# The first half of x squared, normed and turned block by block into eight PSUM banks, with three weight chunks rounded behind it

## The chip, the cores and the metric

The kernel runs on one core of a Trainium2 chip. The metric is the device time of one execution in microseconds, measured on several executions; the lower the better. The core has a matrix engine (PE, whose weight loads the profile lists apart as PEld), a vector engine (DVE), a scalar engine (ACT), a general engine (POOL) and a queue engine that issues most transfers (SP). Each works through its own queue in order and waits at an instruction until what it needs is there. Matrix results go to PSUM, which has eight banks of 128 x 512 f32 values.

## What is computed

One layer of a decoder step: a half-step SwiGLU FFN, a token mixer (a pooling branch and an SSD branch, gated and merged), a second half-step FFN, a last norm, for 1024 prompt tokens and 64 sample tokens of width 1024. The change concerns only the start of the first FFN:

```python
def rmsnorm(x, g):
    xf = x.astype(jnp.float32)
    y = xf * lax.rsqrt(jnp.mean(xf * xf, axis=-1, keepdims=True) + EPS)
    return (y * g.astype(jnp.float32)).astype(x.dtype)

def swiglu(x, w_in, w_out):
    gu = x @ w_in
    g, u = gu[..., :D_FF], gu[..., D_FF:]
    return (jax.nn.silu(g) * u) @ w_out

x = x + 0.5 * swiglu(rmsnorm(x, norm_ffn1[l]), ffn1_w_in[l], ffn1_w_out[l])
```

## The kernel before

**Halves, blocks, k.** The tokens are worked on in two halves: h = 0 has 512 prompt tokens, h = 1 has 512 prompt tokens and the 64 samples. x lies in memory token by token, and the products want it with the channels on the partitions. So `load_x(h, out)` loads a half in blocks of 128 tokens, each as two tiles of 512 channels (`xin`), and turns it on PE: eight slices k of 128 channels, each a PSUM bank (`ptx`) of 128 channels x 512 tokens. The norm rides along: the right operand of the turning matmul is a diagonal matrix `dg` with the reciprocal root mean square of each token.

**Steps of load_x before.** ACT squares all eight tiles and sums each row into `ss` (L911). Then, once for all blocks: DVE adds the two column halves (L914) and scales (L915), POOL takes the power -0.5 (`rsqrt`, L377), DVE makes one diagonal for each block (L921). Then for each k: four turns into one bank (L930), ACT writes the scaled slice `xn` (L934), DVE writes its rounded form `hi` (L935), and `lo = xn - hi` goes to DVE for even k and POOL for odd k (L940). hi and lo of half 0 share a tile named `hl`. Banks come from a pool of eight, split into six of tag `pd` for products and two of tag `ps` for the rest; the turns use `ps`, so at most two slices are under way.

**Products.** Every f32 product is made of three passes on rounded operands: hi x wh, lo x wh, hi x wl. `load_w` (L284) loads a chunk of weights (four slices of k, 128 columns) into `wraw`; ACT rounds it to `wh` (L307) and DVE makes the remainder `wl` (L308). There are three buffers each for `wh` and `wl`. Half 0 does its first three column blocks of the FFN plainly (`ffn_in_plain`, L626), half 1 its first two; for each k the plain code makes six passes, three into `pg` and three into `pu`. The other blocks use a scheme with seven products for a 2 x 2 split, whose operands are sums of slices: `combine` (L508) makes them with subtractions on POOL (L520) and splits them with ACT (L528) and DVE (L529).

**What sets the order.** The program is written as generators ("chains") with due times counted in matmul time; `tick` steps those that are due. Behind that a list scheduler orders each engine's instructions by priority, with a higher priority where the code says `tc.high_priority`, and a semaphore guards each true dependency. `hold` (L280) is a tiny POOL copy out of `ss` into a tile that is about to be loaded; it keeps a load back until that value is there. The second half's x and the weight chunks of k = 4 to 7 are held back in this way by the first half's `ss`.

**The start.** The main program opens the stage, steps `load_x` of half 0 five times, loads the first four weight chunks (`ahead`, the first chunk's key being (0, 0)), then starts `load_x` of half 1.

Of the kernel before, what the change touches and what calls it, by code (L numbers as in the profile page):

```python
# [21 lines left out]
NS = NB * NT  # L22
EPS = 1e-6
# [7 lines left out]
NTOK = (512, 576)  # L31
# [43 lines left out]
def tile_hybrid_pool_ssd_macaron(  # L75
# [10 lines left out]
    V, S, T, G = nc.vector, nc.scalar, nc.tensor, nc.gpsimd  # L86
# [12 lines left out]
    def act(shape=(P, 576), dt=F32, name="a"):  # L99
        return sp.tile(list(shape), dt, tag="act", bufs=N_ACT, name=nm(name))  # L100
# [20 lines left out]
    def fx(dt=F32, name="x"):  # L121
        if stage["name"] == "mix":
            return act((P, 576), dt, name)
        return stage["p"].tile([P, 592], dt, tag="fx", bufs=N_FX, name=nm(name))

    def psum(tag="ps", name="ps"):
        npd = stage["npd"]
        return stage["ps"].tile([P, 512], F32, tag=tag, bufs=npd if tag == "pd" else 8 - npd, name=nm(name))
# [46 lines left out]
    def mm(out, lhsT, rhs, start=True, stop=True, free=False):  # L175
        T.matmul(out, lhsT, rhs, start=start, stop=stop, skip_group_check=free)  # L176
        pe[0] += max(out.free_size(), 64) / 2400.0 * (1 if rhs.dtype == F32R else 4)
# [11 lines left out]
    ident = cp.tile([P, P], F32, tag="ident", name="ident")  # L189
# [50 lines left out]
    late = []  # L240
# [40 lines left out]

        G.tensor_copy(t[:1, :1], src)

    def load_w(w, k0, nk, c0, ncol=P, behind=None, keep=False):  # L284

        if (k0, c0) in ahead:
            return ahead.pop((k0, c0))
        if (w.tensor.name, k0, c0) in parted:
            nth[0] += 1
            out = []  # L290
            for t, src in zip(("wh", "wl"), parted[w.tensor.name, k0, c0]):
                if nth[0] % 2:
                    o = sp.tile([P, 4 * P], F32, tag="wraw", bufs=N_RAW, name=nm(t)).bitcast(F32R)
                else:
                    o = sp.tile([P, 4 * P], F32R, tag=t, bufs=N_W, name=nm(t))
                o = o[:, : nk * P]
                dma(o.bitcast(F32), src)
                out.append(o.rearrange("p (k c) -> p k c", c=ncol))
            return tuple(out)
        raw, wh, wl = (sp.tile([P, 4 * P], d, tag=t, bufs=n, name=nm(t))[:, : nk * ncol]  # L300
                       for t, d, n in (("wraw", F32, N_RAW), ("wh", F32R, N_W), ("wl", F32R, N_W)))
        if behind is not None:
            hold(raw, behind)
        dma(raw.rearrange("p (k c) -> p k c", c=ncol),
            w[k0 * P : (k0 + nk) * P, c0 : c0 + ncol].rearrange("(k p) c -> p k c", p=P))
        with tc.high_priority(hp[0]):
            S.activation(wh, raw, AF.Copy)  # L307
            V.tensor_tensor(wl, raw, wh.bitcast(F32), op=ALU.subtract)  # L308
        if keep:
            to = [dp.tile([P, nk * P], F32, tag=nm("part"), name=nm("part")) for _ in range(2)]  # L310
            for a, b in zip(to, (wh, wl)):
                dma(a, b.bitcast(F32))
            parted[w.tensor.name, k0, c0] = to
        return wh.rearrange("p (k c) -> p k c", c=ncol), wl.rearrange("p (k c) -> p k c", c=ncol)
# [60 lines left out]
    def rsqrt(r, ss):  # L375

        G.tensor_tensor(r, ss, mhalf[: ss.shape[0], : ss.shape[1]], op=ALU.pow)  # L377
# [510 lines left out]
    def load_x(h, out):  # L888


        N = NTOK[h]
        blocks = blocks_of(h)
        nb = len(blocks)
        ss = small((P, 4, 5), "xss", 2)
        if h == 1:
            G.memset(ss, 1.0)
        raws = []
        for src, _, c in blocks:
            raws.append([])
            for q in range(2):  # L900
                t = act((P, 512), name="xin")
                if h == 1:
                    hold(t, late[0][:1, 0, :1])
                dma(t[:c, :], src[:, q * 512 : (q + 1) * 512])
                raws[-1].append(t)
        late.append(ss)
        yield X1_AT if h else 0.2
        for i, (_, c0, c) in enumerate(blocks):
            for q in range(2):
                junk = act((P, 512), name="junk")  # L910
                S.activation(junk[:c], raws[i][q][:c], AF.Square, accum_out=ss[:c, q, i : i + 1])  # L911
            yield 0.5
        v = ss[:, 0, :nb]
        V.tensor_tensor(v, v, ss[:, 1, :nb], op=ALU.add)  # L914
        V.tensor_scalar(v, v, 1.0 / D, EPS, op0=ALU.mult, op1=ALU.add)  # L915
        rsqrt(ss[:, 2, :nb], v)
        yield 0.5
        dg = act((P, 576), name="dg")
        dg = [dg[:, i * P : i * P + b[2]] for i, b in enumerate(blocks)]
        for i, (_, c0, c) in enumerate(blocks):  # L920
            V.tensor_scalar_mul(dg[i][:c, :c], ident[:c, :c], ss[:c, 2, i : i + 1])  # L921
        if h == 1:
            pq = psum("ps", "pxs")
            for k in range(KD):
                mm(pq[:, k * NS : (k + 1) * NS], raws[4][k // 4][:NS, (k % 4) * P : (k % 4 + 1) * P], dg[4][:NS, :NS])
        hi, lo, xn, hl = [None] * KD, [None] * KD, [None] * KD, [None] * KD
        for k in range(KD):
            pt = psum("ps", "ptx")
            for i in range(4):
                mm(pt[:, i * P : (i + 1) * P], raws[i][k // 4][:, (k % 4) * P : (k % 4 + 1) * P], dg[i])  # L930
            x = fx(name="xn") if k >= 4 else act((P, 576), name="xn")
            a, b, both = (act((P, 576), F32R, "hi"), act((P, 576), F32R, "lo"), None) if h else pair(576)
            g = cols[:, i_g1 + k : i_g1 + k + 1]
            S.activation(x[:, :512], pt, AF.Copy, scale=g)  # L934
            V.tensor_scalar_mul(a[:, :512], pt, g)  # L935
            if h == 1:
                ps_ = pq[:, k * NS : (k + 1) * NS]
                S.activation(x[:, 512:N], ps_, AF.Copy, scale=g)
                V.tensor_scalar_mul(a[:, 512:N], ps_, g)
            (G if k % 2 else V).tensor_tensor(b[:, :N], x[:, :N], a[:, :N].bitcast(F32), op=ALU.subtract)  # L940
            hi[k], lo[k], xn[k], hl[k] = a, b, x, both
            yield 0.9
        out.append((h, hi, lo, xn, hl))
# [407 lines left out]
    st = open_stage("ffn1", N_PDF)  # L1351
    finish(start(load_cols(0, nr0)))
    prep1 = [(start(load_x(h, o)), o) for h, o in ((0, []), (1, []))]
    for _ in range(5):
        prep1[0][0].step()
    for kb in (0, 4):
        for c0 in (0, FF):
            ahead[kb, c0] = load_w(wi1, kb, 4, c0, behind=late[0][:1, 0, :1] if kb else None)
    prep1[1][0].step()

    def turn():
# [600 lines left out]
```

## Time and profile before

| what | us |
|---|---|
| median of three runs | 2876.56 (2874.2 to 2882.31) |
| the profiled execution | 2876.81 |
| its span | 2875.0 |
| PE busy | 2777.4 |
| last square of the first half ends, 12.04 + 0.19 | 12.23 |
| first turn on PE | 14.28 |
| first product on PE | 19.80 |
| first turn of the second half (pxs) | 36.77 |
| first plain product of the second half | 75.30 |

The span is the time from the first to the last instruction in the profile; the time of the execution has about 1.8 us more around it. All times in the views are counted from the span's start. In an order of time a row gives the start, the duration, the engine, the line, the operation, the tile written and those read, a count, and in brackets the idle time ahead of it with what ended it.

### The profile page before, as it was taken

How to read it: one execution, taken by the hardware profiler on the slowest of the kernel's cores; microseconds unless marked ns; L12 is line 12 of the kernel's file. 1: busy time of each engine (PE TensorE's matmuls, PEld its weight loads, DVE VectorE, ACT ScalarE, POOL GpSimd, SP SyncE). 2: the span in 40 equal slices, each digit the busy share in tenths (PEclk: the TensorE clock that was granted, in tenths of full speed). 3: DMA queues.
4: the chain of work that ended last, by engine and by line, in shares of the span. 5: the costliest groups of instructions: out<-in, count | busy, mean ns of one | idle time of the engine just before them, and what ended most of it. 6: DMA issues, size and time to landing. Idle time of an engine off the chain costs nothing. (4 is left out here: it accounts for less than half of the span.)

```text
span 2875.0 us, 54724 instructions
## 1 busy us (share of the span) xinstructions
PE 2777.4 (97%) x19834; PEld 2600.5 (90%) x19834; DVE 1887.1 (66%) x2912; ACT 1411.0 (49%) x3150; POOL 1377.5 (48%) x1406
## 2 busy tenths in 40 slices
PE   7999999999999999999999999899999999999998
PEld 5999999899889999999998887678999999998997
DVE  6655565777884586877776777866665544457776
ACT  5444444543454565554556566566233344435433
POOL 5566567543442365554632333333225766664432
PEclk9999999999999999999999999899999999999999
DMA  4565554797745455554367578786675323337865
GB/s 130 185 209 191 175 161 151 248 294 250 238 128 159 152 168 170 176 159 137 99 231 231 188 231 252 231 260 199 226 253 168 121 91 98 99 111 255 289 208 183
DMA packets 515792, 539.50 MB, mean 188 GB/s; under 512 B 41780, under 2 KB 356008, under 8 KB 515512
## 3 DMA queue, kind: packets, MB, share of 16 engines
q1 hardware_dynamic: 515504, 535.99, 58.1%
q8 instruction: 156, 2.56, 0.4%
q14 instruction: 116, 0.95, 0.1%
q10 hardware_dynamic: 16, 0.00, 0.0%
HBM read 383.43 MB, written 152.65 MB: 186 GB/s over the span
## 5 line engine op out<-in xcount | busy, mean ns | idle before, releaser
L176 PE MATMUL pw<-X,wh 128*128 128x288 f32 (+2 forms) x2832 | 626.3, 310 | 4.3 <-ACT v L575 2.7
L176 PEld LDWEIGHTS pw<-X,wh 128*128 128x128 f32 x2832 | 461.5, 189 | 26.4 <-ACT v L575 3.3
L176 PE MATMUL pw<-X,wl 128*128 128x288 f32 (+1 forms) x1644 | 473.1, 288 | 0.6 <-DVE wl L458 0.6
L458 DVE TENSOR_TENSOR wl<-s,wh 128x512 fp32r<-128x512 f32 x288 | 245.8, 855 | 245.2 <-ACT wh L457 232.5
L176 PE MATMUL pw<-hl,wh 128*128 128x256 f32 (+1 forms) x1536 | 393.1, 329 | 3.7 <-ACT t L579 2.5
L451 POOL TENSOR_TENSOR s<-wraw,wraw 128x512 f32<-128x512 f32 x144 | 198.2, 1376 | 330.6 <-DVE wl L458 214.4
L176 PE MATMUL pw<-hi,wh 128*128 128x288 f32 x1120 | 331.7, 296 | 1.8 <-DVE t L615 1.0
L176 PE MATMUL pw<-hi,wl 128*128 128x288 f32 x1120 | 329.8, 294 | 0.0
L176 PE MATMUL pw<-lo,wh 128*128 128x288 f32 x1120 | 329.7, 294 | 0.0
L176 PEld LDWEIGHTS pw<-X,wl 128*128 128x128 f32 x1644 | 311.1, 189 | 0.8 <-DVE wl L458 0.8
L176 PE MATMUL pw<-hl,wl 128*128 128x256 f32 x1072 | 301.4, 281 | 1.2 <-DVE wl L458 1.2
L176 PEld LDWEIGHTS pw<-hl,wh 128*128 128x128 f32 x1536 | 259.5, 190 | 25.3 <-ACT t L579 3.2
L758 POOL TENSOR_TENSOR ws<-wraw,wraw 128x512 f32<-128x512 f32 x120 | 177.5, 1486 | 200.5 <-DMA wraw<-in_ffn_w_out_dram 88.7
L458 DVE TENSOR_TENSOR wl<-wraw,wh 128x512 fp32r<-128x512 f32 x216 | 179.9, 833 | 125.1 <-ACT wh L457 121.4
L457 ACT ACTIVATE wh<-s 128x512 fp32r<-128x512 f32 x288 | 181.0, 629 | 136.1 <-PE pw L176 110.1
L176 PEld LDWEIGHTS pw<-hi,wh 128*128 128x128 f32 x1120 | 210.5, 188 | 8.7 <-DVE t L615 1.7
L457 ACT ACTIVATE wh<-wraw 128x512 fp32r<-128x512 f32 x216 | 135.6, 628 | 154.1 <-PE pw L176 132.8
L176 PEld LDWEIGHTS pw<-lo,wh 128*128 128x128 f32 x1120 | 210.6, 188 | 0.0
L176 PEld LDWEIGHTS pw<-hi,wl 128*128 128x128 f32 x1120 | 210.1, 188 | 0.0
L176 PEld LDWEIGHTS pw<-hl,wl 128*128 128x128 f32 x1072 | 203.8, 190 | 2.2 <-DVE wl L458 2.2
L176 PE MATMUL po<-hh,wh 128*128 128x272 f32 x848 | 178.7, 292 | 8.2 <-ACT wh L766 6.9
L176 PE MATMUL pso<-yhl,wh 128*128 128x288 f32 (+1 forms) x768 | 178.0, 337 | 5.0 <-ACT acc L1752 4.4
(402 smaller groups left out, 6826.8 us busy)
## 6 DMA issues: line engine op xcount, KB each, us to landing
wraw<-in_ffn_w_out_dram SPq DMA_DIRECT2D x240, 256.0 KB
wraw<-in_ffn_w_in_dram SPq DMA_DIRECT2D x188, 256.0 KB
wraw<-in_w_in_dram SPq DMA_DIRECT2D x144, 256.0 KB
wh<-part SPq DMA_DIRECT2D x116, 256.0 KB
wl<-part SPq DMA_DIRECT2D x116, 256.0 KB
hr<-xq SPq DMA_DIRECT2D x106, 272.0 KB
xq<-s SPq DMA_DIRECT2D x66, 272.0 KB
xq<-g SPq DMA_DIRECT2D x62, 272.0 KB
```

The source lines that it names most:

```text
L176: T.matmul(out, lhsT, rhs, start=start, stop=stop, skip_group_check=free)
L451: G.tensor_tensor(t, a, b, op=op)
L457: S.activation(wh, a, AF.Copy)
L458: V.tensor_tensor(wl, a, wh.bitcast(F32), op=ALU.subtract)
L758: G.tensor_tensor(s, raws[0], raws[1], op=ALU.subtract if p in MINUS2 else ALU.add)
```

## The change

Half 0 no longer waits for all its squares. In the order of the blocks, ACT squares a block's two tiles, DVE and POOL make the statistics for that block's single column of `ss`, DVE makes its diagonal, and PE turns all eight slices of this block into eight banks at once: six of tag `pd` and two of tag `ps`. So the eight banks are taken until the slices are read, and the first products take the banks of the first slices. The rest of `load_x` (scaling, hi, lo) becomes a function, `leave_x`, which both halves use; half 1 keeps the old order of work. The first weight chunk is now loaded behind one step of the chain, and the rounding of the second to the fourth chunk is pinned to program order.

```diff
-    def load_w(w, k0, nk, c0, ncol=P, behind=None, keep=False):
+    def load_w(w, k0, nk, c0, ncol=P, behind=None, keep=False, pin=lambda i: i):
...
-            S.activation(wh, raw, AF.Copy)
-            V.tensor_tensor(wl, raw, wh.bitcast(F32), op=ALU.subtract)
+            pin(S.activation(wh, raw, AF.Copy))
+            pin(V.tensor_tensor(wl, raw, wh.bitcast(F32), op=ALU.subtract))
...
         late.append(ss)
         yield X1_AT if h else 0.2
+        if h == 0:
+            pts = [psum("pd" if k < 6 else "ps", "ptx") for k in range(KD)]
+            for i in range(4):
+                cut = slice(i, i + 1)
+                for q in range(2):
+                    junk = act((P, 512), name="junk")
+                    S.activation(junk, raws[i][q], AF.Square, accum_out=ss[:, q, cut])
+                V.tensor_tensor(ss[:, 2, cut], ss[:, 0, cut], ss[:, 1, cut], op=ALU.add)
+                V.tensor_scalar(ss[:, 2, cut], ss[:, 2, cut], 1.0 / D, EPS, op0=ALU.mult, op1=ALU.add)
+                rsqrt(ss[:, 3, cut], ss[:, 2, cut])
+                dg = act((P, P), name="dg")
+                V.tensor_scalar_mul(dg, ident, ss[:, 3, cut])
+                for k in range(KD):
+                    mm(pts[k][:, i * P : (i + 1) * P], raws[i][k // 4][:, (k % 4) * P : (k % 4 + 1) * P], dg)
+                yield 0.5
+            yield from leave_x(h, out, pts, None)
+            return
...
-    for _ in range(5):
+    prep1[0][0].step()
+    first_w = load_w(wi1, 0, 4, 0)
+    for _ in range(4):
         prep1[0][0].step()
+    ahead[0, 0] = first_w
     for kb in (0, 4):
-        for c0 in (0, FF):
-            ahead[kb, c0] = load_w(wi1, kb, 4, c0, behind=late[0][:1, 0, :1] if kb else None)
+        for c0 in (FF,) if kb == 0 else (0, FF):
+            ahead[kb, c0] = load_w(wi1, kb, 4, c0, behind=late[0][:1, 0, :1] if kb else None,
+                                pin=tc.keep_in_program_order)
```

The scheduler's order changes with it, on every engine, up to about a tenth of the program; behind that the rows of every engine are the same again.

On PE, at the start of the program, the rows before were these; xin are the tiles of x, ptx the banks of turned slices, and pg and pu the first products.

```order
L176 MATMUL ptx_527<-dg_502,xin_421 128x128
L176 MATMUL pg_588<-hl_513,wh_442 128x512 x2
L176 MATMUL pg_588<-hl_513,wl_443 128x512
L176 MATMUL ptx_537<-dg_502,xin_409 128x128
L176 MATMUL ptx_537<-dg_502,xin_413 128x128
L176 MATMUL ptx_537<-dg_502,xin_417 128x128
L176 MATMUL ptx_537<-dg_502,xin_421 128x128
L176 MATMUL pu_589<-hl_513,wh_448 128x512
```

With the change, the same place on PE, the last block's turns and the first products, reads:

```order
L176 MATMUL ptx_431<-dg_497,xin_421 128x128
L176 MATMUL ptx_432<-dg_497,xin_421 128x128
...
L176 MATMUL ptx_437<-dg_497,xin_423 128x128
L176 MATMUL ptx_438<-dg_497,xin_423 128x128
L176 MATMUL pg_600<-hl_560,wh_426 128x512
L176 MATMUL pu_601<-hl_560,wh_508 128x512
L176 MATMUL pg_600<-hl_560,wh_426 128x512
L176 MATMUL pg_600<-hl_560,wl_427 128x512
```

Before, the last five slices were turned between products; now all 32 turns stand ahead of the first product, and no turn of this half stands behind it.

On POOL, in the stretch in which PE does the first plain block, the rows before were these; hl written from xn is the lo of an odd k (523 is k = 1, 543 k = 3, 563 k = 5), and the others are subtractions of `combine`.

```order
L940 TENSOR_TENSOR hl_523<-xn_522,hl_523 128x512
L520 TENSOR_TENSOR xn_522<-xn_522 128x256
L520 TENSOR_TENSOR xn_532<-xn_532 128x256
L940 TENSOR_TENSOR hl_543<-xn_542,hl_543 128x512
L520 TENSOR_TENSOR xn_542<-xn_542 128x256
L940 TENSOR_TENSOR hl_563<-xn_562,hl_563 128x512
```

With the change, POOL's rows from the lo of k = 3 (575) to that of k = 5 (585) are:

```order
L966 TENSOR_TENSOR hl_575<-xn_574,hl_575 128x512
L520 TENSOR_TENSOR xn_559<-t_74_615,xn_559 128x256
L520 TENSOR_TENSOR xn_564<-t_84_659,xn_564 128x256
L520 TENSOR_TENSOR xn_569<-xn_569 128x256
L520 TENSOR_TENSOR xn_574<-xn_574 128x256
L520 TENSOR_TENSOR t_102_734<-xn_589,xn_569 128x256
L520 TENSOR_TENSOR xn_569<-t_102_734,xn_569 128x256
L966 TENSOR_TENSOR hl_585<-xn_584,hl_585 128x512
```

One subtraction stood between these two lo; now six do. Four subtractions stand between the lo of k = 1 and that of k = 3 where two stood, and two stand between k = 5 and k = 7.

On ACT, where the second half is squared (junk), the rows before ended like this; wh are rounded weight chunks, X operands of the seven products.

```order
L911 ACTIVATE junk_623,xss_467<-xin_487 128x512
L307 ACTIVATE wh_461<-wraw_460 128x512
L911 ACTIVATE junk_625,xss_467<-xin_490 128x512
L911 ACTIVATE junk_630,xss_467<-xin_493 64x512
L911 ACTIVATE junk_632,xss_467<-xin_496 64x512
L528 ACTIVATE X_645<-xn_512 128x256
L307 ACTIVATE wh_844<-wraw_843 128x512
```

With the change, ACT's rows at the first squares of the second half are:

```order
L307 ACTIVATE wh_521<-wraw_520 128x512
L307 ACTIVATE wh_812<-wraw_811 128x512
L928 ACTIVATE junk_632,xss_527<-xin_529 128x512
L928 ACTIVATE junk_634,xss_527<-xin_532 128x512
L528 ACTIVATE X_638<-xn_559 128x256
L928 ACTIVATE junk_644,xss_527<-xin_535 128x512
L307 ACTIVATE wh_818<-wraw_817 128x512
L928 ACTIVATE junk_646,xss_527<-xin_538 128x512
```

Before, all ten squares of the second half stood ahead of the second block's weights (wh_844); now the second block's two first chunks (wh_812 and wh_818) stand ahead of ten and of seven of them.

More of the change, by code (lines that the diff above doesn't have):

```diff
@@ L921, in load_x, with turned @@
             V.tensor_scalar_mul(dg[i][:c, :c], ident[:c, :c], ss[:c, 2, i : i + 1])
[L922 to L926, printed above, removed]
+        pq = psum("ps", "pxs")
         for k in range(KD):
+            mm(pq[:, k * NS : (k + 1) * NS], raws[4][k // 4][:NS, (k % 4) * P : (k % 4 + 1) * P], dg[4][:NS, :NS])
+        def turned(k):
             pt = psum("ps", "ptx")
@@ L930, in load_x, with leave_x @@
                 mm(pt[:, i * P : (i + 1) * P], raws[i][k // 4][:, (k % 4) * P : (k % 4 + 1) * P], dg[i])
+            return pt
+        yield from leave_x(h, out, turned, pq)
+    def leave_x(h, out, pts, pq):
+        N = NTOK[h]
+        hi, lo, xn, hl = [None] * KD, [None] * KD, [None] * KD, [None] * KD
+        for k in range(KD):
+            pt = pts(k) if h else pts[k]
             x = fx(name="xn") if k >= 4 else act((P, 576), name="xn")
```

## Prediction

> **What bounds the kernel now.** I read the busy shares first, then the span in stages, then the order of time on TensorE (PE) in the first 80 us.
>
> ```profile
> span 2875.0 us, 54724 instructions
> PE 2777.4 (97%) x19834; PEld 2600.5 (90%) x19834; DVE 1887.1 (66%) x2912; ACT 1411.0 (49%) x3150; POOL 1377.5 (48%) x1406
> ```
>
> PE is busy 97% of the span, so the time is PE's work plus its 97.6 us of idle time (2875.0 - 2777.4). The change neither adds nor removes a matmul. It can only move idle time, or time in which the matmuls run slowly. The profiled execution took 2876.81 us, 1.81 us more than its span, and lies 0.25 us above the median of the three runs (2876.56); I add to 2876.8.
>
> The next view is busy time by stretches (stretch, length, busy and count by engine, granted clock, DMA share, GB/s).
>
> ```profile
> core 0: us, PE busy (x) PEld busy (x) DVE busy (x) ACT busy (x) POOL busy (x), PEclk, DMA share, GB/s
> 0.00:14.00 14.00, 0.24 (x1) 0.18 (x1) 1.17 (x5) 8.76 (x20) 3.45 (x22) 1.00 0.83 249
> 34.60:36.80 2.20, 0.17 (x2) 0.06 (x1) 1.17 (x6) 0.00 (x0) 2.20 (x8) 1.00 0.00 0
> 36.80:39.00 2.20, 2.20 (x17) 2.13 (x18) 0.47 (x1) 0.22 (x1) 1.45 (x7) 0.92 0.17 49
> 39.00:42.00 3.00, 3.00 (x12) 2.71 (x12) 0.78 (x2) 0.78 (x2) 0.00 (x0) 0.50 0.37 101
> 42.00:75.30 33.30, 29.97 (x157) 24.48 (x156) 30.12 (x44) 18.16 (x41) 24.80 (x23) 1.00 0.28 75
> 75.30:320.00 244.70, 242.61 (x1658) 228.77 (x1657) 147.42 (x242) 110.49 (x258) 150.49 (x146) 1.00 0.61 195
> ```
>
> Nothing can be won late: from 75.3 to 320 us PE idles 2.1 us, and behind about a tenth of the program the two orders are the same row for row on every engine. What the change can touch lies before 75.3 us: 13.8 us of waiting for x, the gap of 2.0 us at 34.6, three microseconds at half clock behind it (1.5 us lost), and 3.3 us in small gaps later.
>
> **What the change moves forward.** PE's own rows at the start (start, duration, work, idle before):
>
> ```profile
> 14.28 1.22 PE L176 MATMUL ptx<-dg,xin 128*128 128x128 f32 x4 [11.75 <-DVE dg L921]
> 15.68 2.78 PE L176 MATMUL ptx<-dg,xin 128*128 128x128 f32 x12 [0.18 <-DVE dg L921]
> 18.89 1.16 PE L176 MATMUL ptx<-dg,xin 128*128 128x128 f32 x8 [0.43 <-DVE hl L935]
> 19.80 0.71 PE L176 MATMUL pg<-hl,wh 128*128 128x512 f32 x2
> ...
> 33.45 0.61 PE L176 MATMUL pg<-hl,wh 128*128 128x512 f32 x2
> ...
> 34.13 0.61 PE L176 MATMUL pu<-hl,wh 128*128 128x512 f32 x2
> 36.77 1.97 PE L176 MATMUL pxs<-dg,xin 64*128 64x64 f32 x16 [2.03 <-issue]
> ...
> 43.10 1.05 PE L176 MATMUL ptx<-dg,xin 128*128 128x128 f32 x8
> 43.91 0.47 PE L176 MATMUL pg<-hl,wh 128*128 128x512 f32 x1
> ```
>
> An f32 turn (ptx) is two records, so the first half of x has 64. Only 24 are done when the first product starts at 19.80; 40 follow between products. A record costs 0.23 us at the start (2.78 / 12) and 0.10 later (8 from 43.10 to 43.91). A product of 128x512 costs 0.23 (three from 33.45 to 34.13).
>
> The Trainium skill, "TensorE: Matmul & The Clock Gate", part 1 on the HAM clock gate, says that matmuls run at half rate for about 3.4 us of sustained work, and that an idle window of about 3.4 us brings half rate back. Here the slow records last 4.2 us from 14.28 although the row shows no lowered clock, and the clock falls to 0.50 after a gap of 2.2 us. By the page's figure the new first turns would be warm 0.8 us sooner and the estimate below about 0.5 us shorter. I use this trace's own durations.
>
> When can the turns start after the change? From these ACT, POOL and DVE rows:
>
> ```profile
> 7.51 0.19 ACT L911 ACTIVATION_READ_ACCUMULATOR junk<-xin 128x1 f32 x1
> 12.04 0.19 ACT L911 ACTIVATION_READ_ACCUMULATOR junk<-xin 128x1 f32 x1
> 17.36 0.69 ACT L934 ACTIVATE xn<-ptx,cols 128x512 f32<-128x512 f32 x1 [3.36 <-PE ptx L176]
> 12.87 1.03 POOL L377 TENSOR_TENSOR xss<-xss,mhalf 128x4 f32<-128x4 f32 x1 [5.38 <-DVE xss L915]
> 18.08 0.75 DVE L935 TENSOR_SCALAR hl<-ptx,cols 128x512 fp32r<-128x512 f32 x1 [2.07 <-ACT xn L934]
> 18.87 0.69 DVE L940 TENSOR_TENSOR hl<-xn,hl 128x512 fp32r<-128x512 f32 x1
> ```
>
> Sums of squares to first turn took 14.28 - 12.23 = 2.05 us. Block 0's sum is ready at 7.70, so its turns start at 9.75. Three more sets of tiny DVE and POOL operations (add, scale, power, diagonal) lie beside the arrival of x, on engines that stood idle there. The power on one column is not in the trace: it lies between 0.12 us (the tiny POOL copies, ten in 1.24 below) and the 1.03 of four columns; I take 1.03, the same operation. The cheap end starts the turns 0.9 us sooner.
>
> From 9.75 the turns run slowly for 4.2 us, 18 records; the other 30 of blocks 0 to 2 take 3.0 us more, to 16.95. Block 3's diagonal is there by 14.2 as before, so PE itself is last. The first bank is whole at 17.2. Then ACT's xn (0.69), DVE's hi (0.75): k = 0 has its hi at 18.65, k = 1 at 19.4, and k = 0 its lo at 20.1. The first product moves from 19.80 to 18.65, and 40 records at 0.10 no longer stand between products: **a head start of 1.15 + 4.0 = 5.2 us**. The second product waits for DVE's read of bank 1 (19.4), since it takes that bank; PE lives on k = 0 until 20.97.
>
> **What takes it back: POOL.** POOL makes lo for odd k, and the subtractions of `combine`, in one queue.
>
> ```profile
> 6.26 1.24 POOL L282 COPY xin<-xss 1x1 f32<-1x1 f32 x10
> 19.70 0.74 POOL L520 TENSOR_TENSOR xn<-xn 128x256 f32<-128x256 f32 x1 [5.80 <-DVE hl L940]
> 20.39 1.28 POOL L940 TENSOR_TENSOR hl<-xn,hl 128x512 fp32r<-128x512 f32 x1
> ...
> 26.21 1.28 POOL L940 TENSOR_TENSOR hl<-xn,hl 128x512 fp32r<-128x512 f32 x1 [0.25 <-DVE hl L935]
> 27.44 1.90 POOL L520 TENSOR_TENSOR t<-xn,xn 128x256 f32<-128x256 f32 x2
> ...
> 31.08 1.18 POOL L520 TENSOR_TENSOR xn<-t,xn 128x256 f32<-128x256 f32 x1
> 32.23 0.73 POOL L520 TENSOR_TENSOR xn<-xn,t 128x256 f32<-128x256 f32 x1
> 32.92 1.28 POOL L940 TENSOR_TENSOR hl<-xn,hl 128x512 fp32r<-128x512 f32 x1
> ```
>
> POOL has no pause from 19.70 to 34.20. A lo costs 1.28, a subtraction 0.73 to 1.18; I take 0.94, near the middle (the pair at 27.44 has 0.95 each). Before, k = 5's lo is the third lo behind four subtractions (done at 27.49). In the new order ten subtractions stand before it. POOL's first lo can start at 19.4, when k = 1 has its hi. So lo of k = 3 ends at 19.4 + 2 x 1.28 + 4 x 0.94 = 25.7, of k = 5 at 25.7 + 6 x 0.94 + 1.28 = 32.6, of k = 7 at 35.8.
>
> PE takes six products, 1.38 us, for each k. It reaches k = 3's lo at 24.0 and waits 1.7; it reaches k = 5's at 28.45 and **waits 4.2 us**; k = 7's comes at 35.8. By then 43 products are done. Before, 41 were done at 34.6. The head start is gone.
>
> **The second half's squares.** ACT's next chunk (`wh` for block 1's u) stands ahead of seven of the ten squares and needs the buffer that PE reads until 36.05. Then 0.63 for that copy, seven squares at 0.70, two operands at 0.40 and a read of 0.19 end at 42.6. The statistics take 1.9 (12.23 to 13.94, the power at 1.21), five diagonals 1.05:
>
> ```profile
> 34.38 1.21 POOL L377 TENSOR_TENSOR xss<-xss,mhalf 128x5 f32<-128x5 f32 x1 [0.17 <-DVE xss L915]
> 35.63 1.05 DVE L921 TENSOR_SCALAR dg<-ident,xss 128x128 f32<-128x128 f32 x5 [1.06 <-POOL xss L377]
> ```
>
> So the samples' turns (pxs) start at 45.5 where they started at 36.77, but behind 76 products instead of 41. The 35 products are worth 8.05, so this mark is 45.5 - 8.05 - 36.77 = 0.7 us late. Clock: before, the gap at 34.6 was followed by half clock, about 1.6 us lost (1.5 at 39 to 42 and a little before it). After, a gap of 4.2 us should do the same; part of that lies within the wait for k = 7, so I add 1.3. **Sum: +0.7 + 1.3 - 1.6 = +0.4 us.** Without the drop it is -0.9.
>
> Unknown prices move this: subtractions at 0.73 take 2.5 us off (12 of them), at 1.18 they add 2.9; the cheap power takes 0.9 off.
>
> **DMA.** The second half's ten loads are let go by POOL's tiny copies, now behind the fourth power (about 15 instead of 7.5); SP issued them from 11.46 to 17.9 before, and now sends a weight chunk and a state copy ahead. ACT asks for the first of them only behind two weight copies at about 28, a cover of over 8 us. If it were gone, each microsecond late would be one on pxs. The pinned order of the three weight copies costs nothing: they stand where they stood, behind the eighth square.
>
> **Rivals.**
> - *The head start is kept* (0.20). If POOL's subtractions run at 0.73 and the power is short, the waits shrink and PE may stay at full clock: -0.9 - 2.5 - 0.9 gives 2872.5. At most all of 5.2, the gap of 2.03 and the lost 1.6 are won: 2868. For it: POOL's price varies by 60%. Against: six subtractions stand between two lo that PE needs 2.8 us apart.
> - *DVE falls behind* (0.20), the slower side. DVE's part of the second half starts 8.7 us later, with two weight remainders and three operands (about 4.3 us, at 0.9 and 0.8) done early. From 36.8 to 75.3 it was busy 0.47 + 0.78 + 30.12 = 31.4 of 38.5 us, and a weight remainder kept PE waiting:
>
> ```profile
> 70.82 0.50 PE L176 MATMUL pu<-hl,wl 128*128 128x512 f32 x1 [2.10 <-DVE wl L308]
> ```
>
>  From 45.5 to 75.3 it would need 27.1 of 29.8 us. If its queue keeps the 7.1 us of waits that it had, it ends 4.3 us late, and PE with it when the second half's plain blocks start: 2881.5. It decides once DVE's waits there pass 2.7 us. At worst the whole 8.7 shows: 2885.5.
> - *The change does not act* (0.05): if the first turns wait for PE's banks or the last diagonal after all, the time stays 2876.8. The new order speaks against it; no row stands between prow and the turns.
>
> **How the numbers follow.** The forecast, the head start given back (0.55), is 2876.8 + 0.4 = 2877.2, by itself between 2873 and 2881. With both rivals' ends the range is 2868 to 2885. A change of this kernel is told from none at about 0.3%, 8.6 us. Only the far end of the first rival is faster by that (0.05) and the far end of the second slower (0.07); 0.88 lies within.
>
> **What would show it.** Right: turns from about 9.7, the first product near 18.7, a wait of PE for POOL of some 4 us near 28 to 33, a low clock just after, no gap at 34.6, and pxs near 45 to 47. Wrong: no such wait at k = 5, or PE waiting for DVE's hi or wl for more than 5 us between 47 and 80. Work that differs beyond 320 us would make the whole frame wrong.

## Result and the profile after

The changed kernel took 2902.68 us (median of four executions, 2898.45 to 2910.54), the kernel before beside it 2879.43 (2874.2 to 2885.47). The ratio is 1.008, 95% interval 1.0064 to 1.0095: some 23 us slower, and outside the range of the prediction.

The profiled execution of the changed kernel took 2902.49 us. Its first lines, the busy times:

```profile
span 2900.7 us, 54726 instructions
PE 2796.8 (96%) x19834; PEld 2617.4 (90%) x19834; DVE 1883.1 (65%) x2918; ACT 1412.0 (49%) x3150; POOL 1380.8 (48%) x1409
```

PE has 6.3 us more idle time (103.9 against 97.6) and 19.4 us more busy time for the same 19834 records. So most of the loss is matmuls that ran slowly: in the trace's record of the granted clock, half clock adds up to 97.9 us, before to 53.1 (means of 0.983 and 0.991). The matmul of the same number on PE stands later than before by this much (after minus before, us). Up to number 1966 the two orders differ in places, so there it need not be the same product:

| matmul number | time before | late by |
|---|---|---|
| 100 | 33.2 | 0.2 |
| 300 | 76.8 | 1.9 |
| 400 | 90.3 | 8.6 |
| 500 | 103.8 | 9.2 |
| 700 | 133.4 | 12.6 |
| 1300 | 223.3 | 15.0 |
| 1500 | 253.8 | 17.8 |
| 2100 | 343.8 | 19.5 |
| last (19834) | | 25.7 |

Almost nothing is lost where the prediction looked, and 17.6 us between 76.8 and 343.8 us, which it took to be out of the change's reach. First the start. PE's order of time in the changed kernel, its long waits only:

```profile
17.64 0.50 PE L176 MATMUL pg<-hl,wh 128*128 128x512 f32 x1
...
25.23 0.50 PE L176 MATMUL pg<-hl,wh 128*128 128x512 f32 x1 [2.17 <-POOL hl L966]
...
32.31 0.50 PE L176 MATMUL pg<-hl,wh 128*128 128x512 f32 x1 [2.56 <-POOL hl L966]
...
45.73 2.59 PE L176 MATMUL pxs<-dg,xin 64*128 64x64 f32 x16 [0.84 <-issue]
...
86.31 0.53 PE L176 MATMUL pu<-hi,wh 128*128 128x288 f32 x2 [1.80 <-ACT wh L307]
...
89.42 0.85 PE L176 MATMUL pu<-hi,wl 128*128 128x288 f32 x2 [2.31 <-DVE wl L308]
...
141.79 0.40 PE L176 MATMUL pw<-hi,wh 128*128 128x288 f32 x1 [2.50 <-ACT t L613]
...
234.11 0.50 PE L176 MATMUL pw<-hl,wh 128*128 128x512 f32 x1 [1.88 <-DVE t L581]
...
261.07 0.41 PE L176 MATMUL pw<-hi,wh 128*128 128x288 f32 x1 [1.93 <-DVE t L615]
...
352.42 0.40 PE L176 MATMUL pw<-hi,wh 128*128 128x288 f32 x1 [1.61 <-DVE t L615]
```

The first four rows are the predicted ones. The last six are new: two waits in the second half's first plain block, then four in the blocks behind (`pw`), at 142, 234, 261 and 352 us. Busy time by stretches shows what each costs (length, busy and count by engine, granted clock):

```profile
80.00:100.00 20.00, 15.89 (x100) 15.42 (x100) 14.51 (x21) 6.92 (x17) 9.87 (x10) 0.83 0.36 111
87.80:94.60 6.80, 5.18 (x21) 5.18 (x22) 3.14 (x4) 0.00 (x0) 2.15 (x3) 0.50 0.37 116
142.50:145.90 3.40, 3.40 (x14) 3.21 (x13) 2.68 (x5) 0.25 (x1) 1.46 (x2) 0.50 0.74 220
100.00:400.00 300.00, 291.46 (x1939) 273.16 (x1938) 169.44 (x271) 129.19 (x296) 189.97 (x181) 0.98 0.57 184
```

and the kernel before in the two long stretches:

```profile
80.00:100.00 20.00, 19.92 (x148) 19.47 (x147) 12.19 (x22) 7.11 (x16) 5.85 (x4) 1.00 0.47 140
100.00:400.00 300.00, 297.61 (x2009) 279.30 (x2008) 177.45 (x281) 135.44 (x309) 193.27 (x187) 1.00 0.59 189
```

In the 20 us from 80 on PE does 100 matmuls instead of 148. It idles 4.1 us, and for 6.8 us, the last 1.6 us of the second wait among them, the clock is halved. From 100 to 400 us it idles 8.54 us instead of 2.39, and three more stretches at half clock follow the waits.

### The profile page after: what moved, and what is told of

Read it like the earlier page. It is cut to its first block, busy times and chain, and to the rows that moved or that the text cites. A ratio compares the mean times of both kernels' runs of the same rounds, so it can differ in the third digit from the quotient of the medians.

```text
span 2900.7 us, 54726 instructions
## 1 busy us (share of the span) xinstructions
PE 2796.8 (96%) x19834; PEld 2617.4 (90%) x19834; DVE 1883.1 (65%) x2918; ACT 1412.0 (49%) x3150; POOL 1380.8 (48%) x1409
## 3 DMA queue, kind: packets, MB, share of 16 engines
q8 instruction: 156, 2.56, 0.4%
## 5 line engine op out<-in xcount | busy, mean ns | idle before, releaser
L176 PE MATMUL po<-hh,wl 128*128 128x272 f32 x848 | 178.1, 292 | 6.0 <-DVE wl L767 5.8
```

## What the change moved by accident

The program's own clock explains where these two losses could come from. `mm` books each matmul on that clock, an f32 turn at 512 / 2400 = 0.213. Before, the five steps of `load_x` that run ahead of everything else end with the last square, and no turn is booked when the next three chains are started with their due times: the second half's squares (`X1_AT` 4.0), the turns of the state into `xr` (`TURN_AT` 60) and the constants (`CONST_AT` 40). After the change these five steps hold all 32 turns. So the clock stands 32 x 0.2133 = 6.827 further when the three are started, and each falls due 6.83 later in the work that follows. The diff has no line that says so. The order shows it beyond the first half's stage: with tile numbers and line numbers taken off, PE's records in the two profiles differ up to number 1966 of 19834, at 341 us.

That gives **theory A**: the shift of due times is the loss. **Theory B** is its rival: the turning itself and the pinned weight copies leave DVE and POOL late, and the later waits follow from that.

## First experiments: the due times

`a_due` puts all three back, `a_x1` the first alone, `a_tc` the other two; `b_due` makes the shift alone, in the kernel before.

```diff
 a_due                                      b_due (in the kernel before)
-X1_AT = 4.0                               -X1_AT = 4.0
+X1_AT = -2.827                            +X1_AT = 10.827
-TURN_AT, CONST_AT = 60.0, 40.0            -TURN_AT, CONST_AT = 60.0, 40.0
+TURN_AT, CONST_AT = 53.173, 33.173        +TURN_AT, CONST_AT = 66.827, 46.827
```

> The changed kernel, with the three due times of the work that is started before the first half's products (second half's squares X1_AT 4.0, turns of the state TURN_AT 60, constants CONST_AT 40) each lowered by 6.827, the price that the program's own clock books for the 32 turns (32 x 512/2400). Theory A (the program's clock): the change books the turns of the first half before these three are started, so that they fall due 6.83 later in the work, and this shift is what costs. A expects the rows behind the first half's stage to come back to those of before, no stretch of half clock between 80 and 400 us, and a time within 5 us of the kernel before (ratio 0.998 to 1.002). Theory B (the turning itself): turning block by block and the pinned weight copies leave DVE and POOL late, and the later waits follow from that; B expects the waits near 86 to 90, 142, 234 and 261 us to stay and the ratio at 1.006 to 1.009.

> The changed kernel with X1_AT alone lowered by 6.827 (the second half of x is due where it was in the work; the state's turns and the constants stay 6.83 late). Theory A splits the loss: the late second half costs the 6 to 7 us between 76 and 99 us, the late turns of the state the rest, 12 to 14 us from 142 us on. A expects 6 to 9 us less than the changed kernel (ratio 1.004 to 1.006), no wait for wl or wh near 86 to 90, and the waits near 142, 234, 261 and 352 us still there. Theory B expects nothing to change (1.006 to 1.009).

> The changed kernel with TURN_AT and CONST_AT alone lowered by 6.827 (second half of x still late). Theory A: the waits of 1.8 and 2.3 us near 86 to 90 and the half clock behind them stay (6 to 7 us), those near 142, 234, 261 and 352 us go (12 to 14 us): ratio 1.002 to 1.004. A rival within A: the later waits hang on the second half's lateness and not on the state's turns; then this kernel is as slow as the changed one (1.006 to 1.009) and the one with X1_AT alone is near 1.000. Theory B: 1.006 to 1.009.

> The kernel before, with nothing of the change, but the three due times each raised by 6.827. Theory A: the shift alone is the loss, so it is 16 to 24 us slower than the kernel before (ratio 1.005 to 1.009) with PE's waits near 80 to 100, 142 and 234 to 262 us as in the changed kernel. Theory B: no more than 4 us from the kernel before (0.9985 to 1.0015).

| kernel | median us | ratio to before (95%) | PE idle 80 to 100 us | PE idle 100 to 400 us |
|---|---|---|---|---|
| changed kernel | 2902.68 | 1.0080 (1.0064 to 1.0095) | 4.11 | 8.54 |
| a_due (all three back) | 2880.10 | 1.0012 (1.0002 to 1.0021) | 0.82 | 2.32 |
| a_x1 (X1_AT back) | 2897.22 | 1.0061 (1.0045 to 1.0078) | 3.37 | 9.89 |
| a_tc (TURN_AT, CONST_AT back) | 2879.12 | 1.0006 (0.9997 to 1.0016) | 0.47 | 2.56 |
| b_due (shift in the kernel before) | 2890.01 | 1.0039 (1.0024 to 1.0054) | 1.99 | 9.73 |

Theory B falls as the whole cause: with the due times back and all of the change in place, the kernel is within 0.2% of before. What it names has a part in the early loss, as the next section shows. Theory A holds in the main, but its split was wrong. I had put the early waits down to the late second half; they stay in `a_x1` (one wait of 3.37 us at 88.2) and go in `a_tc`, where the second half is as late as in the changed kernel. So both losses hang on `TURN_AT` and `CONST_AT`. The shift alone costs the kernel before 0.4% (13 us, where 16 to 24 were forecast), with the loss behind 100 us in full and of the early loss only a part (one wait of 1.56 us). a_due lies a little above before: its interval leaves up to 0.2% to the change itself.

## Second experiments: two losses, two causes

In the order, `CONST_AT` alone moves one pair of weight copies on ACT and DVE, besides the constants' own rows. `TURN_AT` moves the rows of the state's turns: the loads (`xin2` in the code, `xin` in the profile), the turns `ptr` and their copies `xr`, and with them some neighbours on ACT, DVE and POOL.

```diff
-TURN_AT, CONST_AT = 60.0, 40.0
+TURN_AT, CONST_AT = 60.0, 33.173     a_const
+TURN_AT, CONST_AT = 53.173, 40.0     a_turn
+TURN_AT, CONST_AT = 62.173, 40.0     a_turn9
...
-PART_AT, PART_W, PART_PACE = 20.0, 6.0, 3.0
+PART_AT, PART_W, PART_PACE = 20.0, 9.0, 3.0     a_partw
```

> The changed kernel with CONST_AT alone lowered by 6.827. On ACT and DVE this moves one pair of weight copies (wh, wl, L307 and L308) from behind six of the second half's operands (X, L528 and L529) to ahead of them, as in the kernel before; apart from the copies of the constants themselves nothing else moves. Theory A1 (two losses with two causes): the waits near 86 and 89 us and the half clock behind them go, the waits near 142, 234, 261 and 352 us stay: 6 to 8 us less than the changed kernel, ratio 1.004 to 1.006. Rival (only the state's turns matter, the early waits come from the late second half): no change, 1.007 to 1.009.

> The changed kernel with TURN_AT alone lowered by 6.827. Theory A1: the waits near 86 and 89 us stay, those near 142, 234, 261 and 352 us go, 10 to 14 us less than the changed kernel: ratio 1.002 to 1.005. Rival (the late second half alone makes the early waits and the constants' place makes none): same as that. Rival (each wait has a cause of its own): some of the four stay.

> The changed kernel with TURN_AT at 62.173, so one period of turn_x (7 + 2 on the program's clock) behind the value of 53.173 that restores the old place. Theory of the phase: turn_x and part both have a period of 9, so what counts is how xin2 and pr stand to each other in SP's order; with the same phase the four waits near 142 to 352 us go although the turns are later even than in the changed kernel: ratio 1.002 to 1.005, as with TURN_AT lowered. Theory of lateness: the turns stand 2.2 later than in the changed kernel, so the waits stay or grow: 1.007 to 1.011.

> The changed kernel with PART_W raised from 6 to 9, so that ph (L369) is put 3 later behind its load pr (L322). Theory of the load: in all four waits ACT stands at ph until pr lands (140.30, 232.10, 259.24, 350.64 us) while PE's next evacuation is queued behind it; with 3 more of distance the four waits go or shrink below 1 us, the early waits near 86 to 90 us stay: 8 to 13 us less than the changed kernel, ratio 1.003 to 1.005. Rival (ACT or DVE themselves are too late, the load only happens to be last): no change or a shift of the waits to other places, 1.006 to 1.010.

| kernel | median us | ratio to before (95%) | PE idle 80 to 100 us | PE idle 100 to 400 us |
|---|---|---|---|---|
| a_const | 2890.83 | 1.0042 (1.0027 to 1.0057) | 0.08 | 10.07 |
| a_turn | 2885.20 | 1.0027 (1.0017 to 1.0037) | 4.11 | 3.96 |
| a_turn9 | 2891.91 | 1.0041 (1.0026 to 1.0056) | 4.09 | 6.51 |
| a_partw | 2892.74 | 1.0049 (1.0032 to 1.0067) | 4.10 | 5.12 |

`a_const` and `a_turn` separate the two losses: each takes away its own idle time, all or most of it, and leaves the other's. Of the four later waits `a_turn` keeps one (1.94 us at 252.7, without half clock behind it). `a_turn9` is undecided: three of the four are gone and that at 142 is down to 1.22 us, as the phase would have it, but a new one of 3.62 us stands at 169.5, so a turn one period later is not the same as the old place. `a_partw` makes the waits smaller (1.94 at 142, 1.39 at 166, 1.03 at 256) and another 6.9 us are lost between matmuls 2600 and 4000 (420 to 621 us), 2.4 of which come back. The chain runs longer there, but that this is the reason isn't shown: three stretches of 3.41 us at half clock lie there (at 526, 570 and 635 us), and at 563 to 581 us such a stretch stands also in `a_const`, `a_turn` and `b_dve` (a run further down), whose PE order there is that of before.

**The early loss.** DVE's order of time in the changed kernel:

```profile
80.01 1.06 DVE L529 TENSOR_TENSOR X<-xn,X 128x288 fp32r<-128x288 f32 x1
80.99 1.29 DVE L308 TENSOR_TENSOR wl<-wraw,wh 128x512 fp32r<-128x512 f32 x1
82.21 1.07 DVE L529 TENSOR_TENSOR X<-xn,X 128x288 fp32r<-128x288 f32 x1
83.20 1.06 DVE L529 TENSOR_TENSOR X<-t,X 128x288 fp32r<-128x288 f32 x1
84.19 2.04 DVE L529 TENSOR_TENSOR X<-xn,X 128x288 fp32r<-128x288 f32 x2
86.15 1.05 DVE L529 TENSOR_TENSOR X<-t,X 128x288 fp32r<-128x288 f32 x1
87.12 1.04 DVE L529 TENSOR_TENSOR X<-xn,X 128x288 fp32r<-128x288 f32 x1
88.09 1.27 DVE L308 TENSOR_TENSOR wl<-wraw,wh 128x512 fp32r<-128x512 f32 x1
```

and in `a_const`, whose time there is about 1 us later:

```profile
82.44 1.28 DVE L308 TENSOR_TENSOR wl<-wraw,wh 128x512 fp32r<-128x512 f32 x1
84.85 0.86 DVE L308 TENSOR_TENSOR wl<-wraw,wh 128x512 fp32r<-128x512 f32 x1 [1.13 <-ACT wh L307]
85.64 0.26 DVE L227 COPY cols<-prow 128x112 f32<-128x112 f32 x1
85.82 0.88 DVE L529 TENSOR_TENSOR X<-xn,X 128x288 fp32r<-128x288 f32 x1
```

In the changed kernel six operands of the second half stand between the two remainders `wl`, and PE waits for the second (89.42). (The wait at 86.31 is for its rounding `wh`, which ACT does behind the same operands.) DVE has no idle time there; an operand takes some 1.05 us beside POOL's subtractions of `combine`, and 0.44 without them. In the kernel before those subtractions were done by 78.70 us, in the changed kernel by 90.03:

```profile
88.78 1.25 POOL L520 TENSOR_TENSOR xn<-xn,t 128x288 f32<-128x288 f32 x1
```

The row itself is not new. In the kernel before `wl` stands behind seven operands, 0.44 us each now that POOL is done, and PE didn't wait for it (it needed the copy at 83.11):

```profile
76.97 1.07 DVE L529 TENSOR_TENSOR X<-xn,X 128x288 fp32r<-128x288 f32 x1
77.96 1.29 DVE L308 TENSOR_TENSOR wl<-wraw,wh 128x512 fp32r<-128x512 f32 x1
79.18 0.44 DVE L529 TENSOR_TENSOR X<-xn,X 128x288 fp32r<-128x288 f32 x1
...
81.20 0.81 DVE L529 TENSOR_TENSOR X<-xn,X 128x288 fp32r<-128x288 f32 x2
81.94 1.28 DVE L308 TENSOR_TENSOR wl<-wraw,wh 128x512 fp32r<-128x512 f32 x2
```

So the early loss takes two things at once: the row behind the operands and POOL's lateness, which is theory B's part. `a_const` takes away the first. It puts the `wl` ahead of the six, a place that it doesn't have in the kernel before either (the expectation had that wrong), and nothing is lost although POOL is as late (its last subtraction ends at 91.32). Why the scheduler gives the copies that place when the constants move was not tested.

**The later loss.** ACT's order of time ahead of two of the four waits, in the changed kernel:

```profile
135.15 0.60 ACT L579 COPY t<-pw 128x512 f32<-128x512 f32 x1
140.30 0.63 ACT L369 ACTIVATE ph<-pr 128x512 fp32r<-128x512 f32 x1 [4.55 <-DMA pr<-in_ffn_w_in_dram]
140.84 0.61 ACT L457 ACTIVATE wh<-wraw 128x512 fp32r<-128x512 f32 x1
141.35 0.38 ACT L613 COPY t<-pw 128x288 f32<-128x288 f32 x1
...
259.24 0.63 ACT L369 ACTIVATE ph<-pr 128x512 fp32r<-128x512 f32 x1 [5.25 <-DMA pr<-in_ffn_w_in_dram]
```

`ph` is a rounding for a later stage (`part`), which PE doesn't need for a long time. But it stands in ACT's queue ahead of the evacuation L613 (a copy out of PSUM) that PE needs, and it waits for its load `pr`. At 234, 261 and 352 us it is the same one engine on: `ph`, then `pr` (L371) on DVE, then DVE's evacuation. SP's order of time ahead of the first, in the changed kernel:

```profile
135.07 0.38 SPq L477 DMA_DIRECT2D wraw<-in_ffn_w_in_dram  x1
135.55 0.46 SPq L977 DMA_DIRECT2D xin<-in_x_prompt_dram  x1
136.10 0.38 SPq L322 DMA_DIRECT2D pr<-in_ffn_w_in_dram  x1
```

and in the kernel before:

```profile
124.95 0.38 SPq L477 DMA_DIRECT2D wraw<-in_ffn_w_in_dram  x1
125.43 0.45 SPq L322 DMA_DIRECT2D pr<-in_ffn_w_in_dram  x1
...
129.56 0.34 SPq L951 DMA_DIRECT2D xin<-in_x_prompt_dram  x1
```

The state's load has slipped ahead of `pr`, which lands at 140.30, 4.2 us after its issue. But the slip is some 0.5 us, too little for a wait of 2.50. In the kernel before ACT stands as long at the same `ph`, and PE waits for the same evacuation, only less:

```profile
129.77 0.63 ACT L369 ACTIVATE ph<-pr 128x512 fp32r<-128x512 f32 x1 [4.72 <-POOL s L676]
...
131.43 0.41 PE L176 MATMUL pw<-hi,wh 128*128 128x288 f32 x1 [0.75 <-ACT t L613]
```

There `ph` starts 4.3 us after the issue of `pr` as well. What has changed is how early `pr` goes out. PE was ready for that product at 130.68 (131.43 - 0.75) in the kernel before, 5.25 us after the issue, and at 139.29 in the changed kernel, 3.19 us after it. So `pr` is 2.1 us later against PE: 0.5 by the state's load, and 1.5 because the weight load `wraw` ahead of both is itself later. That 1.5 goes with the late turns (`pr` goes out 5.27 us ahead in `a_turn`, and 3.06 in `b_turn`, a run further down with `TURN_AT` alone raised), but its way through the queues was not taken apart.

## Third experiments: the two mechanisms taken apart

`a_t5` moves little but the weight copies' rows, `a_nopart` takes `ph` and `pr` out, `b_turn` makes only the state's turns late in the kernel before.

```diff
-            c = start(first(gen), T_AT)
+            c = start(first(gen), T_AT + (5.0 if prep is prep1 and h else 0.0))     a_t5
...
-    ffn(wi1, ffn1_w_out[0], prep1, after1, side=side())
+    ffn(wi1, ffn1_w_out[0], prep1, after1)     a_nopart
...
-TURN_AT, CONST_AT = 60.0, 40.0
+TURN_AT, CONST_AT = 66.827, 40.0     b_turn (in the kernel before)
```

> The changed kernel; the second half's combine is started 5 later on the program's clock (7 instead of 2). PE's rows stay the same, and on ACT and DVE nothing moves but two pairs of weight copies (wh, wl), which come ahead of three to five of the second half's operands (X). Theory of the row: the waits of 1.80 and 2.31 us near 86 and 89 us come from the place of these copies behind the operands, not from the constants; they go or fall below 1 us, the four waits near 142 to 352 us stay: 5 to 8 us less than the changed kernel, ratio 1.004 to 1.006. Rival (the operands come too late anyway, with POOL 11 us behind): the wait moves to the products that need X, and the time stays at 1.007 to 1.009.

> The changed kernel without part: the chain that loads, rounds and stores weights of later stages beside this stage is left out (those weights are rounded later, where they are used), so no pr and no ph stands in SP's, ACT's and DVE's queues. Theory of the load: with ph gone none of the four waits near 142, 234, 261 and 352 us is left, and from 100 to 400 us PE loses under 2 us against the kernel before (the changed kernel lost 10.9 there); the early waits near 86 to 90 us stay. Rival (xin2 and its copies of the turned state hold the queues by themselves): waits of 1.5 us or more stay at two or more of these places. The total time is open, since the rounding left out comes back in the later stages.

> The kernel before with TURN_AT alone raised by 6.827. Theory of the load: the late turns of the state are enough, without anything of the change, so that PE waits near 131, 225, 250 and 342 us for evacuations queued behind ph: 10 to 14 us slower, ratio 1.003 to 1.005, with nothing lost before 100 us. Rival (the waits need the second half's lateness or the block-wise turning as well): within 3 us of the kernel before.

| kernel | median us | ratio to before (95%) | PE idle 80 to 100 us | PE idle 100 to 400 us |
|---|---|---|---|---|
| a_t5 | 2893.64 | 1.0055 (1.0041 to 1.0068) | 0.20 | 11.09 |
| a_nopart | 2905.69 | 1.0095 (1.0079 to 1.0110) | 4.12 | 0.33 |
| b_turn | 2886.06 | 1.0033 (1.0019 to 1.0046) | 0.12 | 9.68 |

All three go with the mechanism. In `a_t5` PE's rows are those of the changed kernel; weight copies and operands change places, and two of POOL's subtractions; the early loss is gone (0.20 us idle). In `a_nopart` none of the four waits is left:

```profile
100.00:400.00 300.00, 299.67 (x2035) 282.38 (x2034) 159.97 (x261) 126.28 (x289) 192.06 (x188) 1.00 0.41 133
```

PE does 2035 matmuls in these 300 us, 26 more than before the change. The bill for the rounding left out comes behind 1810 us, and the total is the slowest of all. In `b_turn` nothing of the change is there and nothing is lost before 100 us. Then ACT shows the same rows:

```profile
131.05 0.63 ACT L369 ACTIVATE ph<-pr 128x512 fp32r<-128x512 f32 x1 [4.62 <-DMA pr<-in_ffn_w_in_dram]
131.59 0.61 ACT L457 ACTIVATE wh<-wraw 128x512 fp32r<-128x512 f32 x1
132.11 0.38 ACT L613 COPY t<-pw 128x288 f32<-128x288 f32 x1
```

PE's waits of 2.69, 3.49 and 2.21 us at 132.5, 249.3 and 341.4 us follow; the 500th matmul was 0.2 us early, the 2100th is 10.1 late.

## What the change itself is worth

With the due times back two questions are left: what the pin does, and whether the head start that POOL takes back can be kept. `a_nopintc` and `a_dvetc` start from `a_tc`; `b_dve` makes the second edit in the kernel before.

```diff
-            ahead[kb, c0] = load_w(wi1, kb, 4, c0, behind=late[0][:1, 0, :1] if kb else None,
-                                pin=tc.keep_in_program_order)
+            ahead[kb, c0] = load_w(wi1, kb, 4, c0, behind=late[0][:1, 0, :1] if kb else None)     a_nopintc
...
-            (G if k % 2 else V).tensor_tensor(b[:, :N], x[:, :N], a[:, :N].bitcast(F32), op=ALU.subtract)
+            (G if k % 2 and h else V).tensor_tensor(b[:, :N], x[:, :N], a[:, :N].bitcast(F32), op=ALU.subtract)     a_dvetc, b_dve
```

> The changed kernel with TURN_AT and CONST_AT restored and without the pin of the three weight copies, which then stand two blocks earlier on ACT and DVE, ahead of the third block's squares. If the pin is worth something, the copies wait there for their chunks to land and hold up the squares behind them: the turns' last block and the first product come 0.5 to 3 us later. If it is worth nothing, the first product stays within the spread of 17.6 to 19.5 us seen so far and the time within 0.2% of the kernel before.

> The changed kernel with TURN_AT and CONST_AT restored (as in the run with both lowered, ratio 1.0006), and the four remainders lo of the first half's odd k made on DVE instead of POOL. Theory of POOL's chain: PE's two waits for POOL (2.1 and 4.1 us near 25 and 32 us) and the half clock behind them go, 6 to 8 us of the head start are kept until the 200th product, and the time is 2 to 6 us below the kernel before (0.998 to 0.9995). Rival (DVE is then late with wl and the second half's operands): the waits move to DVE between 36 and 100 us and the ratio is 1.000 to 1.003.

> The kernel before with only the four remainders lo of the first half's odd k on DVE instead of POOL. With the change and its due times restored this edit gave 0.9977 of the kernel before. Theory of the chain (POOL's remainders ate the head start that the block-wise turning makes): before the change there is no head start to eat and PE waits only 2.0 us there (pxs at 36.77), so the edit alone wins at most 3.5 us (the gap and the half clock behind it): ratio 0.9985 to 1.001. Rival (the remainders on POOL alone are what costs, the turning is worth nothing): 0.9965 to 0.9985, as with the change.

| kernel | median us | ratio to before (95%) |
|---|---|---|
| a_nopintc | 2880.93 | 1.0008 (0.9998 to 1.0018) |
| a_dvetc | 2870.98 | **0.9977 (0.9968 to 0.9986)** |
| b_dve | 2876.83 | 0.9995 (0.9986 to 1.0003) |

The pin is worth nothing that these runs can tell. `a_dvetc` beats the kernel before by 0.23%, and with it the changed kernel. What PE waits for most from 14 to 80 us (us in total, times, the longest), in `a_tc`:

```profile
PE pg L176 <- POOL hl L966: 6.2, 2, 4.1
```

and in `a_dvetc`:

```profile
PE pg L176 <- DVE wl L308: 2.3, 1, 2.3
```

The 6.2 us for POOL are gone, and a wait of 2.3 for a weight remainder has come. At the 300th matmul `a_dvetc` is 4.6 us ahead of the kernel before, `a_tc` 4.4 behind. The edit alone (`b_dve`) can't be told from no change, though its profile was 2.6 us ahead at matmul 200: one jump of 5.5 us near 560 us, with 6.8 us at half clock, took that back, where PE's order is the same in both. So with lo on DVE in both, the turning is worth some 5 us (0.9977 against 0.9995; the two intervals just meet, so the size is loose), and without that POOL's queue ate it.

## Why the prediction was wrong

**Right: the start, in its mechanism.** The turns began at 7.96 instead of 9.75 and took 9.68 us, where the prediction's prices (18 records in 4.2 us, 46 at 0.10) give 8.8: 22 of the 64 records were slow.

```profile
7.96 9.68 PE L176 MATMUL ptx<-dg,xin 128*128 128x128 f32 x64 [5.14 <-DVE dg L919]
```

Of the early start 0.46 us is the power on one column (0.57 instead of 1.03). Most of the rest belongs to this execution: in the eleven runs above that share the start the turns began at 8.67 to 9.66 and the first product came at 18.13 to 19.47, here at 17.64 (predicted 18.65). pxs was due at 45.5 and came at 45.73, in the eight runs that leave `X1_AT` and POOL's lo as the change has them at 46.35 to 48.24. PE waited for POOL's lo twice, 2.17 and 2.56 us where 1.7 and 4.2 were named; in the eight the waits are 2.14 to 2.18 and 2.47 to 4.06. The gap at 34.6 was gone. So POOL eats the head start as was argued, and `a_dvetc` shows it.

The sum for this stage, +0.4 us, agrees with what the change costs when its side effect is undone: 1.0006 and 1.0012 are +2 and +3 us, with +0.4 inside the first interval. But it can't be told so finely. The first plain product of the second half came 1.1 us late here, and between 1.4 us early and 3.6 late in the ten other runs with lo on POOL; that the sum comes so near is in part luck.

**Wrong: the frame.** The step that failed is "Nothing can be won late: from 75.3 to 320 us PE idles 2.1 us, and behind about a tenth of the program the two orders are the same row for row on every engine", from which it follows there that the change can touch only what lies before 75.3 us. The premises are true of the traces and don't bear that conclusion. Little idle time bounds what can be won there, not what can be lost. And I didn't look at what differed within that first tenth, where 19.5 of the profile's 25.7 us were lost. Two shifted due times were enough: `CONST_AT` for the early part (6.7 us between matmuls 300 and 400), `TURN_AT` for the later one (about 10 us up to 344 us).

**The rival "DVE falls behind"** was nearer than the forecast. It named the engine, the late start of its second half and a weight remainder that PE waits for. It had the place wrong: DVE kept up until 75 us (the first plain product of the second half came 1.1 us late) and held PE up 10 us later. And lateness alone was not enough. With the same lateness and other rows (`a_const`, `a_t5`, `a_tc`) nothing was lost, and with the old row and no lateness (the kernel before) nothing either. The price of an operand beside POOL, 1.05 instead of 0.44 us, was not in its sum.

**The clock term.** I priced a drop to half clock once, for 1.3 us, in the first 50 us. There were three stretches by 54 us, 13.65 us in all against 3.41 before. Six later waits of 1.6 to 2.5 us, 12.0 us in all, came with some 17 us at half clock (6.8 and three times 3.4). PE was busy in 15.4 of these, so that some 8 us were lost on top.

**Open.** From 400 us to the end the changed kernel lost another 6 us in its profile, where PE's order is the same as before. The granted clock goes with it: behind 400 us PE stood at half clock for 67.2 us, against 49.7 before, and half of that difference is 8.7 us. `b_due`, with the same order there, made up 7 us against before and stood at half clock for 39.1. What sets off these stretches in one execution and not in another was not looked into, so this part can't be put down to the change.

## What to carry over

When a program books its own time, moving work ahead of a `start` moves every due time behind it; compare the whole order of both kernels on every engine, SP's too, and price the places that differ, however far from the edit. A busy engine with little idle time can lose a lot: ask of each in-order queue which early-placed instruction with a slow load (here `ph`) stands ahead of what the busy engine needs next, and how long before that need the load goes out. A row that does no harm in one kernel can do it in another, as the `wl` behind the operands did once POOL was late. When a head start disappears, find the queue that eats it and move a part of its work: that was worth more here than the change.

## What the runs showed of the hardware

A short wait can cost nearly double: 1.9 to 2.5 us of waiting, and another 1.7 us when 3.41 us at half clock follow. Up to 400 us, in all sixteen profiles, every stretch at half clock was 3.41 us long or twice that. In the changed kernel waits of 1.80 and 2.31, 2.50, 1.88 and 1.93 us led to one; but the wait of 1.61 at 352 us did not, nor did 2.69 at 132.5 in `b_turn`:

```profile
131.00:137.00 6.00, 4.46 (x31) 4.29 (x32) 4.22 (x7) 2.55 (x6) 2.30 (x4) 1.00 0.81 260
```

The Trainium skill, "TensorE: Matmul & The Clock Gate", part 1, has a free-running window of 3413 ns and names an idle window of that length as what brings half rate. The length of the low stretches agrees, and a window that runs freely fits that the same wait drops the clock at one time and not at another. That single waits of 1.88 and 1.93 us were enough differs from the page, and the runs decide.

At the start the views show a clock of 1.00 while the turns run slowly. That is no reading: the trace's record of the clock begins at 18.18 us in the kernel before and at 12.75 in the changed kernel, just where the records of the turns go from 0.21 to 0.11 us apart. From the first turn to there it took 3.9 and 4.8 us, and in the sixteen profiles 3.9 to 6.1. So part of the spread of the start lies in this stretch.

A DVE subtraction of 128x288 took 1.07 us while POOL worked through its own (76.97 in the kernel before, in the rows shown with the early loss) and 0.44 when POOL was idle (79.18, after POOL's last one ended at 78.70).

The Trainium skill, "SBUF — State Buffer", section "SBUF: two separate sides", says that Vector and GPSIMD contend on a port that they share. These rows agree. It makes the place of POOL's work matter for DVE even where neither waits for the other: the six operands of the early loss took 6.3 us at this price and would have taken some 2.6 at the other, by estimate (6 x 0.44).
